# Half of the lower weight parts in the last four stages: from a VectorE subtraction to an accumulating transfer

## The chip, the cores and the metric

The kernel runs on one core of a Trainium2 chip. The metric is the device time of one execution in microseconds (us). The kernel before took 1247.65 us, the median of two runs (1247.44 and 1247.87).

## The reference

One decoder layer on 256 tokens of 2048 features in float32. After an rmsnorm, one wide projection `w_in` feeds a gated convolution branch, a gated linear attention branch with 4 heads and a cross attention into 256 memory tokens. Each branch ends in a projection of its own, is weighted with a sigmoid gate, and the sum goes through `w_out`, the residual and a last rmsnorm:

```
y_conv = (u * silu(conv_z)) @ w_conv_out + b_conv_out
y_gla  = (o * silu(gla_z)) @ w_gla_out
y_mem  = (om * silu(mz)) @ w_mem_out
g = sigmoid(gate_pre + b_gate)          # three gates per feature, from w_in
y = g[0] * y_conv + g[1] * y_gla + g[2] * y_mem
x = x + y @ w_out
return rmsnorm(x, final_g)
```

Nearly all arithmetic is in products of 256 token rows with weight matrices, some 235 MB of float32 weights in all, each read once.

## The kernel before

**Weights and their split.** The host lays the weights out in memory in the order in which the kernel asks for them. A *chunk* is 2 tiles of 128 input features by 512 output columns: 128 partitions of 4 KB, 512 KB in all. `chunk` (L123) loads it into `raw` by a transfer on SP's queue (L139), ScalarE rounds it to its upper 12 significant bits, `hi` (L140, type fp32r), and VectorE subtracts, `lo = raw - hi` (L141). The activations are split in the same way. `mm3` (L157) then makes three matmuls for each product, (upper, upper), (upper, lower) and (lower, upper), lines L158 to L160.

**Buffers.** There are 4 `raw` buffers (NRAW) and 5 each of `hi` and `lo` (NHL). A `hi` or `lo` buffer comes free when the matmuls of the chunk five before are done; a `raw` buffer when its subtraction is done. A few chunks of the last group (`spare=True`) take `hi` and `lo` from another pool.

**Order.** The order on each engine is made by the framework's scheduler, from program order and a simulated timeline. The three lines of a chunk have a raised priority (`tc.high_priority(offset=AHEAD)`, 400 instructions), so that loads and splits run as far ahead as buffers allow. Each engine, and each engine's queue of transfers, then runs its own list strictly in order: an instruction that waits holds up all that stand behind it.

**Groups and stages.** `group_t` (output features on partitions) makes 24 matmuls of 256 columns for a chunk, `group_n` (tokens on partitions) 12 of 512 columns. A group runs over 16 feature tiles, which are 8 chunks, k = 0, 2, ..., 14. Side work (convolution taps, attention heads, norms) is put between chunks. The last four stages, 128 of the chunks, have little of it:

- `cz`: 4 groups for conv_z, each followed by silu, a product and a split;
- `gc` and `yc`: in `merge`, in turn, 4 times one group for the gate (`gc`: bias, sigmoid) and one for `w_conv_out` (`yc`: bias, product, sum into `y`). After each pair `y` is transposed on TensorE and split;
- `out`: 4 groups for `w_out`. The residual `x` and `final_g` are loaded shortly before on SP's queue (L861, L864). In the last group the second half of the tokens runs 12 feature tiles behind the first, so that the end of the first half is covered; its chunks k = 4 and 6 are the `spare` ones.

GpSimd (POOL) issues no transfer in this kernel; it does a few memsets and powers.

Of the kernel before, what the change touches and what calls it, by code (L numbers as in the profile page):

```python
# [8 lines left out]
F32 = mybir.dt.float32  # L9
F32R = mybir.dt.float32r  # L10
U8 = mybir.dt.uint8
AF = mybir.ActivationFunctionType
ALU = mybir.AluOpType
# [3 lines left out]
P = 128  # L17
# [5 lines left out]
CK = 2  # L23
# [25 lines left out]

# columns of the packed per-feature vectors  # L50
V_LN, V_MLN, V_CG, V_CB, V_DB, V_GN, V_BA = 0, 16, 32, 48, 64, 80, 96
# [4 lines left out]
def trunk_kernel(ctx, tc, streamed, xt, memt, x, weights, w_alpha2, vecs, taps, b_gate, b_conv_out,  # L56
# [25 lines left out]

    # ---- side work: generators that are advanced between the chunks of weights. They yield how much
    # work they gave the vector engine, or ("wait", n) to go on n chunks later. ----
    class Side:
# [4 lines left out]
    def start(gen, rank=1):  # L90
        """Tasks of a lower rank go first."""
        task = [gen, 0, rank]
        at = len(Side.queue)
        while at and Side.queue[at - 1][2] > rank:
            at -= 1
        Side.queue.insert(at, task)
        return task
# [26 lines left out]

# [1 line left out]
    def chunk(w, k, a, cols, name, spare=False):  # L126
        """Rows of a tiles of 128 features from tile k on, cols: (first, count) side by side. The weights
        lie in memory in the order in which they are asked for."""
        b = sum(n for _, n in cols)
        at = sum(P * a * sum(n for _, n in cols) for _, _, a, cols in streamed)  # L130
        streamed.append((w, k, a, cols))
        raw = wp.tile([P, a, b], F32, name=f"raw_{name}", tag="raw", bufs=NRAW)
        if spare:
            hi, lo = b4([P, a, b], f"hi_{name}", F32R), b4([P, a, b], f"lo_{name}", F32R)
        else:
            hi = wp.tile([P, a, b], F32R, name=f"hi_{name}", tag="hi", bufs=NHL)
            lo = wp.tile([P, a, b], F32R, name=f"lo_{name}", tag="lo", bufs=NHL)
        with tc.high_priority(offset=AHEAD):
            nc.sync.dma_start(raw, weights[at:at + P * a * b].rearrange("(p k c) -> p k c", p=P, k=a))  # L139
            nc.scalar.copy(hi, raw)  # L140
            nc.vector.tensor_sub(lo, raw, hi.bitcast(F32))  # L141
        return hi, lo
# [19 lines left out]
    def group_t(w, c0, acts, nk, name, first=CK):  # L162
        """Output features on partitions: two tiles of [128, 2, tokens]."""
        pss = [mm_tile(f"pt_{name}_{j}") for j in range(2)]
        for k, hi, lo, ah, al in chunks(w, c0, nk, acts, name, first):
            for n in range(4):
                cols = slice(n * P, (n + 1) * P)
                mm3(pss[n // 2][:, (n % 2) * T:(n % 2 + 1) * T], hi[:, cols], lo[:, cols], ah, al,
                    k == 0 and n % 2 == 0, k == nk - 1)
        return [p.rearrange("p (a b) -> p a b", a=2) for p in pss]  # L170

    def group_n(w, c0, acts, nk, name):
        """Tokens on partitions: one tile of [128, 512], or of the columns, per token tile."""
        n = sum(c[1] for c in c0) if isinstance(c0, list) else GC
        pss = [mm_tile(f"pn_{name}_{t}")[:, 0:n] for t in range(NT)]
        for k, hi, lo, ah, al in chunks(w, c0, nk, acts, name):
            for t in range(NT):
                tok = slice(t * P, (t + 1) * P)
                mm3(pss[t], ah[:, tok], al[:, tok], hi, lo, k == 0, k == nk - 1)
        return pss  # L180
# [9 lines left out]
    def quarters(hi, lo):  # L190
        """Operands of 16 tiles of 128 features, four to a tile of SBUF."""
        return lambda k: (hi[k // 4][:, k % 4, :], lo[k // 4][:, k % 4, :])

    def rms_scale(ss, n, name, w=1):
        """(ss / n + EPS) ** -0.5"""
        ms = tp.tile([P, w], F32, name=f"ms_{name}", tag="ms")
        nc.vector.tensor_scalar(ms, ss, 1.0 / n, EPS, op0=ALU.mult, op1=ALU.add)
        rs = tp.tile([P, w], F32, name=f"rs_{name}", tag="rs")
        nc.gpsimd.tensor_tensor(rs, ms, mhalf[:, 0:w], op=ALU.pow)
        return rs  # L200

    def token_bcast(col, r, name):
        """[tokens, 1] per token tile -> r, [128, tokens], the same row on each partition."""
        pt = aux_tile(f"bc_{name}")
        for t in range(NT):
            dg = t1([P, P], f"dg_{name}_{t}")
            nc.vector.tensor_scalar_mul(dg, ident, col[:, t:t + 1])
            nc.tensor.matmul(pt[:, t * P:(t + 1) * P], lhsT=ones, rhs=dg, start=True, stop=True,
                             skip_group_check=True)
        nc.vector.tensor_copy(r, pt[:, 0:T])  # L210

    def feat_sum(src, name):
        """Sum over partitions of [128, tokens] -> PSUM [tokens, 1] per token tile."""
        pt = aux_tile(f"fs_{name}")
# [5 lines left out]
    def square_sum(part, src, name, squared=False):  # L220
        """part (or None) + the sum of squares over the 4 feature tiles of src."""
        sq = src
# [8 lines left out]

# [1 line left out]
    ones = const.tile([P, P], F32, name="ones")  # L233
# [14 lines left out]

# [1 line left out]
    def raw_operand(src, v0, name, keep):  # L250
        """Loads and splits as it is asked for: the operands, the loaded tiles or their squares."""
        hi, lo, raw, rest = [], [], [], []
# [71 lines left out]

# [1 line left out]
    conv = []  # L326
# [72 lines left out]
    def silu_psum(pz, name):  # L399
        """silu of a PSUM tile."""  # L400
        sg = t2([P, GC], f"sz_{name}")
# [5 lines left out]

# [1 line left out]
    cum = []  # L409

    def decay(alr):
        """alr: per token tile the low-rank inputs, in columns 0 and 64 on the upper, 32 on the lower bits."""
        wa = b4([P, 1024], "wa")
# [15 lines left out]
        for i in range(2):  # L429
            zb = b4([P, 4 * T], f"zb{i}")  # L430
            e = b4([P, 4 * T], f"lse{i}")
            for h in range(2):
# [9 lines left out]
                yield 0.7  # L442
            # log_sigmoid(z) = min(z, 0) - ln(1 + exp(-|z|)); sums inside chunks of TAU * log_a
            nc.scalar.activation(e, zb, AF.Abs)
# [24 lines left out]
    def gla_head(h, q, k, v):  # L469
        """q, k: [128, 2, tokens] of the head, q scaled; v: per token tile [128, 512]."""  # L470
        while len(cum) <= h:
# [3 lines left out]
        qf = q.rearrange("p a b -> p (a b)")  # L475
        # Scores are made as [key, query] for the two token tiles at once. The second tile has its keys
        # in reverse order, so that in each block its lower half lies where the first has its upper one.
        ck = b4([P, 4 * T], f"ck{h}")
# [11 lines left out]
        s1 = t1([P, P], f"s1{h}")  # L490
        # the diagonal, where nothing decays, and pairs of neighbours, where only the query does
        qq = b4([P, 4, P + CHUNK], f"qq{h}")
# [31 lines left out]

        # key in the lower and query in the upper half of a block of 2 L tokens: both decays
        # are taken to the end of the lower half, so that no exponent is positive
        made = []
        for li, L in list(enumerate(LEVELS))[1:]:
# [18 lines left out]
            if len(made) > LAG:  # L547
                level_scores(*made.pop(0))
                yield 0.2
        # key in the first, query in the second half of the sequence  # L550
        kd = t1([P, 2, P], f"kd{h}")
# [28 lines left out]
        yield "wait", 2  # L580
        # o = scores @ v, and its rmsnorm
        ov = b4([P, NT, DVH], f"on{h}")
# [35 lines left out]
    def v_group(h, q, k):  # L618
# [5 lines left out]
        else:  # L624
            # together with the low-rank inputs of the decays
            n = (DVH + RANK) // 2
# [15 lines left out]

# [1 line left out]
    def memory_groups():  # L644
# [77 lines left out]

# [1 line left out]
    def gated_gla():  # L724
        """The normalized o times silu(z), transposed, times the gain of the norm, split."""
        hi, lo = [], []
# [41 lines left out]

# [1 line left out]
    y = []  # L770
# [40 lines left out]

# [1 line left out]
    norm = start(x_norm())  # L813
# [41 lines left out]

# [1 line left out]
    res = []  # L857
# [8 lines left out]
    def residual(po, n, t):  # L866
        """Adds x; the mean of the squares goes to fss, the gain of the final norm to res."""
        half = slice(n % 2 * GC, (n % 2 + 1) * GC)
# [32 lines left out]

    # the last columns: the second token tile ends HELD feature tiles after the first
    pss = [mm_tile(f"pn_out3_{t}") for t in range(NT)]
# [59 lines left out]
```

## Time and profile before

| what | value |
|---|---|
| median of the runs | 1247.65 us |
| lowest and highest run | 1247.44, 1247.87 us |
| span of the profiled execution | 1246.8 us |
| TensorE (PE) busy | 1231.0 us, 99% |
| VectorE (DVE) busy | 964.0 us, 77% |
| ScalarE (ACT) busy | 591.8 us, 47% |
| GpSimd (POOL) busy | 18.6 us, 1% |
| mean share of the 16 DMA engines | some 57%, 191 GB/s |
| HBM read | 235.06 MB |

No time of its own is given for the profiled execution beside its span; the two runs lie 0.6 and 1.1 us above the span, which is the start and the end around it. Busy times are shares of the whole span and average over unlike stages. A matmul's record is longer than the step to the next matmul, since matmuls overlap, so a full PE row says that work was always in flight, not how fast it was.

### The profile page before, as it was taken

How to read it: one execution, taken by the hardware profiler on the slowest of the kernel's cores; microseconds unless marked ns; L12 is line 12 of the kernel's file. 1: busy time of each engine (PE TensorE's matmuls, PEld its weight loads, DVE VectorE, ACT ScalarE, POOL GpSimd, SP SyncE). 2: the span in 40 equal slices, each digit the busy share in tenths (PEclk: the TensorE clock that was granted, in tenths of full speed). 3: DMA queues.
4: the chain of work that ended last, by engine and by line, in shares of the span. 5: the costliest groups of instructions: out<-in, count | busy, mean ns of one | idle time of the engine just before them, and what ended most of it. 6: DMA issues, size and time to landing. Idle time of an engine off the chain costs nothing.

```text
span 1246.8 us, 18825 instructions
## 1 busy us (share of the span) xinstructions
PE 1231.0 (99%) x7338; PEld 1093.9 (88%) x7338; DVE 964.0 (77%) x1502; ACT 591.8 (47%) x711; POOL 18.6 (1%) x29
## 2 busy tenths in 40 slices
PE   7999999999999999999999999999999999999997
PEld 7999899988998998889988888888999888888885
DVE  7999999699999667999699979964565554655553
ACT  7534676446553454444445445544354444444442
POOL 0000000000020000000000000000000000000000
PEclk9999999999999999999999999999999999999999
DMA  7565745446545445665465555565555655567562
GB/s 272 186 191 170 236 153 195 155 161 221 188 165 193 159 152 183 205 204 193 161 218 171 200 201 171 179 228 194 195 183 190 202 202 195 205 227 268 187 215 71
DMA packets 71672, 238.37 MB, mean 191 GB/s; under 512 B 7792, under 2 KB 12144, under 8 KB 71584
## 3 DMA queue, kind: packets, MB, share of 16 engines
q1 hardware_dynamic: 71440, 237.13, 56.6%
q8 instruction: 57, 0.93, 0.3%
q14 instruction: 31, 0.25, 0.1%
q10 hardware_dynamic: 144, 0.05, 0.0%
HBM read 235.06 MB, written 2.10 MB: 190 GB/s over the span
## 4 chain that ended last, share of the span: by engine, by line
PE 97%; DMA 1%; DVE 1%; issue 0%; SPq 0%; ACT 0%; POOLq 0%; DVEq 0%; POOL 0%
PE pt_cb L158 2%; PE pt_cz L158 2%; PE pt_cb L159 2%; PE pt_cb L160 2%; PE pt_cz L159 2%; PE pt_cz L160 2%; PE pn_gc L159 2%; PE pn_gm L159 2%; PE pn_gz L158 2%; PE pn_go L159 2%; PE pn_go L158 2%; PE pn_gm L158 2%; PE pn_gz L159 2%; PE pn_yo L158 2%; PE pn_go L160 2%; PE pn_gc L160 2%
## 5 line engine op out<-in xcount | busy, mean ns | idle before, releaser
L359 DVE SCALAR_TENSOR_TENSOR conv<-u,tap,conv 128x256 f32<-128x256 f32 x480 | 207.3, 474 | 0.0
L158 PE MATMUL pt_ca<-xh,hi_ca 128*128 128x256 f32 x256 | 72.7, 289 | 6.1 <-ACT xh L187 5.1
L159 PE MATMUL pt_ca<-xl,hi_ca 128*128 128x256 f32 x256 | 73.5, 288 | 0.2
L160 PE MATMUL pt_ca<-xh,lo_ca 128*128 128x256 f32 x256 | 72.7, 287 | 0.9 <-DVE lo_ca L141 0.9
L158 PE MATMUL pt_cb<-xh,hi_cb 128*128 128x256 f32 x256 | 72.4, 283 | 0.0
L141 DVE TENSOR_TENSOR lo_yc<-raw_yc,hi_yc 128x1024 fp32r<-128x1024 f32 x32 | 39.2, 1225 | 42.9 <-ACT hi_yc L140 42.9
L160 PE MATMUL pt_cz<-xh,lo_cz 128*128 128x256 f32 x256 | 71.9, 281 | 0.0
L158 PE MATMUL pt_cz<-xh,hi_cz 128*128 128x256 f32 x256 | 71.9, 281 | 0.0
L159 PE MATMUL pt_cz<-xl,hi_cz 128*128 128x256 f32 x256 | 71.9, 281 | 0.0
L160 PE MATMUL pt_cb<-xh,lo_cb 128*128 128x256 f32 x256 | 71.8, 282 | 0.0
L159 PE MATMUL pt_cb<-xl,hi_cb 128*128 128x256 f32 x256 | 71.8, 281 | 0.0
L141 DVE TENSOR_TENSOR lo_cz<-raw_cz,hi_cz 128x1024 fp32r<-128x1024 f32 x32 | 39.2, 1224 | 35.7 <-ACT hi_cz L140 35.7
L141 DVE TENSOR_TENSOR lo_gc<-raw_gc,hi_gc 128x1024 fp32r<-128x1024 f32 x32 | 39.1, 1223 | 34.2 <-ACT hi_gc L140 34.2
L141 DVE TENSOR_TENSOR lo_out<-raw_out,hi_out 128x1024 fp32r<-128x1024 f32 x32 | 39.0, 1224 | 31.5 <-ACT hi_out L140 31.2
L140 ACT CAST hi_gc<-raw_gc 128x1024 fp32r<-128x1024 f32 x32 | 33.6, 1052 | 50.3 <-PE pn_yc L160 24.9
L140 ACT CAST hi_yc<-raw_yc 128x1024 fp32r<-128x1024 f32 x32 | 33.7, 1053 | 49.5 <-PE pn_gc L160 33.4
L140 ACT CAST hi_yo<-raw_yo 128x1024 fp32r<-128x1024 f32 x32 | 33.6, 1051 | 46.7 <-PE pn_go L160 23.4
L141 DVE TENSOR_TENSOR lo_yo<-raw_yo,hi_yo 128x1024 fp32r<-128x1024 f32 x32 | 38.8, 1221 | 21.6 <-ACT hi_yo L140 21.6
L158 PEld LDWEIGHTS pt_ca<-xh,hi_ca 128*128 128x128 f32 x256 | 49.5, 196 | 6.4 <-ACT xh L187 5.1
L140 ACT CAST hi_gm<-raw_gm 128x1024 fp32r<-128x1024 f32 x32 | 33.6, 1050 | 45.2 <-PE pn_gm L160 24.6
L140 ACT CAST hi_go<-raw_go 128x1024 fp32r<-128x1024 f32 x32 | 33.7, 1052 | 44.6 <-PE pn_yo L160 24.6
L140 ACT CAST hi_cz<-raw_cz 128x1024 fp32r<-128x1024 f32 x32 | 33.6, 1050 | 44.3 <-PE pt_cz L159 36.0
(352 smaller groups left out, 4108.9 us busy)
## 6 DMA issues: line engine op xcount, KB each, us to landing
raw_cb<-in_weights SPq DMA_DIRECT2D x32, 512.0 KB, 3.5
raw_gm<-in_weights SPq DMA_DIRECT2D x32, 512.0 KB, 3.2
raw_gz<-in_weights SPq DMA_DIRECT2D x32, 512.0 KB, 3.3
raw_go<-in_weights SPq DMA_DIRECT2D x32, 512.0 KB, 3.6
raw_yo<-in_weights SPq DMA_DIRECT2D x32, 512.0 KB, 3.2
raw_cz<-in_weights SPq DMA_DIRECT2D x32, 512.0 KB, 3.2
raw_gc<-in_weights SPq DMA_DIRECT2D x32, 512.0 KB, 3.2
raw_yc<-in_weights SPq DMA_DIRECT2D x32, 512.0 KB, 3.2
```

Source lines behind the costliest of these rows:

```text
L140: nc.scalar.copy(hi, raw)
L141: nc.vector.tensor_sub(lo, raw, hi.bitcast(F32))
L158: nc.tensor.matmul(o, lhsT=ah, rhs=bh, start=first, stop=False, skip_group_check=True)
L159: nc.tensor.matmul(o, lhsT=ah, rhs=bl, start=False, stop=False, skip_group_check=True)
L160: nc.tensor.matmul(o, lhsT=al, rhs=bh, start=False, stop=last, skip_group_check=True)
L359: nc.vector.scalar_tensor_tensor(acc, u[:, i, j:j + T], tap[:, c, j:j + 1], acc, op0=ALU.mult, op1=ALU.add)
```

## The change

`lo_by` names, for the four last stages, the chunks with k divisible by 4, which is every second one (k = 0, 4, 8, 12 of each group). In `gc` and `out` ("twice") such a chunk is loaded by a transfer from GpSimd's queue straight into `hi`, with the conversion to fp32r on the way; ScalarE writes `lo = -hi`; then a second transfer from GpSimd's queue reads the same weights again and adds them to `lo`. In `cz` and `yc` ("once") `raw` is loaded and `hi` made as before, ScalarE writes `lo = -raw` in fp32r, and a transfer from GpSimd's queue adds the weights to `lo`. A `spare` chunk stays as it was. All other lines of the diff take out comments.

```
+    def lo_by(name, k):
+        if k % (2 * CK):
+            return None
+        if name.startswith(("gc", "out")):
+            return "twice"
+        if name.startswith(("cz", "yc")):
+            return "once"
+        return None
...
     def chunk(w, k, a, cols, name, spare=False):
...
+        src = weights[at:at + P * a * b].rearrange("(p k c) -> p k c", p=P, k=a)
+        how = lo_by(name, k)
+        if how and not spare:
+            hi = wp.tile([P, a, b], F32R, name=f"hi_{name}", tag="hi", bufs=NHL)
+            lo = wp.tile([P, a, b], F32R, name=f"lo_{name}", tag="lo", bufs=NHL)
+            with tc.high_priority(offset=AHEAD):
+                if how == "twice":
+                    nc.gpsimd.dma_start(hi, src)
+                    nc.scalar.activation(lo, hi.bitcast(F32), AF.Copy, scale=-1.0)
+                else:
+                    raw = wp.tile([P, a, b], F32, name=f"raw_{name}", tag="raw", bufs=NRAW)
+                    nc.sync.dma_start(raw, src)
+                    nc.scalar.copy(hi, raw)
+                    nc.scalar.activation(lo, raw, AF.Copy, scale=-1.0)
+                nc.gpsimd.dma_start(lo, src, accum_op=ALU.add)
+            return hi, lo
         raw = wp.tile([P, a, b], F32, name=f"raw_{name}", tag="raw", bufs=NRAW)
...
-            nc.sync.dma_start(raw, weights[at:at + P * a * b].rearrange("(p k c) -> p k c", p=P, k=a))
+            nc.sync.dma_start(raw, src)
             nc.scalar.copy(hi, raw)
             nc.vector.tensor_sub(lo, raw, hi.bitcast(F32))
         return hi, lo
```

## Rows read from the trace of the kernel before

**Rows 1.** The page: busy time of engines; then the chain that ended last, by engine.
```profile
PE 1231.0 (99%) x7338; PEld 1093.9 (88%) x7338; DVE 964.0 (77%) x1502; ACT 591.8 (47%) x711; POOL 18.6 (1%) x29
...
PE 97%; DMA 1%; DVE 1%; issue 0%; SPq 0%; ACT 0%; POOLq 0%; DVEq 0%; POOL 0%
```

**Rows 2.** Busy time by windows: three stretches of loads, then four short ones.
```profile
core 0: us, PE busy (x) PEld busy (x) DVE busy (x) ACT busy (x) POOL busy (x), PEclk, DMA share, GB/s
862.00:972.00 110.00, 110.00 (x854) 106.53 (x854) 61.65 (x62) 48.36 (x54) 0.00 (x0) 1.00 0.56 189
972.00:1150.00 178.00, 178.00 (x798) 147.03 (x797) 100.74 (x103) 76.85 (x82) 0.00 (x0) 1.00 0.64 218
1150.00:1219.00 69.00, 69.00 (x310) 57.23 (x309) 43.55 (x46) 32.98 (x41) 0.00 (x0) 1.00 0.57 192
1115.00:1126.00 11.00, 11.00 (x51) 9.06 (x49) 6.10 (x6) 4.36 (x6) 0.00 (x0) 1.00 0.96 339
1137.00:1148.00 11.00, 11.00 (x50) 9.13 (x49) 4.90 (x4) 4.38 (x5) 0.00 (x0) 1.00 0.79 290
1126.00:1137.00 11.00, 11.00 (x50) 9.04 (x50) 6.10 (x6) 5.29 (x7) 0.00 (x0) 1.00 0.79 244
1060.00:1071.00 11.00, 11.00 (x54) 9.14 (x53) 8.36 (x11) 4.87 (x6) 0.00 (x0) 1.00 0.64 222
```

**Rows 3.** The page's groups: busy us, mean ns | idle before, its releaser; the split.
```profile
L141 DVE TENSOR_TENSOR lo_yc<-raw_yc,hi_yc 128x1024 fp32r<-128x1024 f32 x32 | 39.2, 1225 | 42.9 <-ACT hi_yc L140 42.9
...
L141 DVE TENSOR_TENSOR lo_gc<-raw_gc,hi_gc 128x1024 fp32r<-128x1024 f32 x32 | 39.1, 1223 | 34.2 <-ACT hi_gc L140 34.2
...
L140 ACT CAST hi_gc<-raw_gc 128x1024 fp32r<-128x1024 f32 x32 | 33.6, 1052 | 50.3 <-PE pn_yc L160 24.9
```

**Rows 4.** Timeline (start, length, idle before): casts, a subtraction, and the matmul that uses lo.
```profile
983.69 1.05 ACT L140 CAST hi_yc<-raw_yc 128x1024 fp32r<-128x1024 f32 x1 [1.70 <-PE pn_gc L160]
984.77 1.23 DVE L141 TENSOR_TENSOR lo_yc<-raw_yc,hi_yc 128x1024 fp32r<-128x1024 f32 x1 [1.52 <-ACT hi_yc L140]
986.43 1.05 ACT L140 CAST hi_yc<-raw_yc 128x1024 fp32r<-128x1024 f32 x1 [1.70 <-PE pn_gc L160]
...
994.66 0.39 PE L159 MATMUL pn_yc<-lo_yc,uh 128*128 128x512 f32 x1
```

**Rows 5.** Tile raw_gc: issue on SP (ns min/median/max), and its transfers' landing.
```profile
L139 SPq DMA_DIRECT2D raw_gc<-in_weights x32: 327/328/328, 952.5 to 1105.3; - x32
...
DMA to landing us min/median/max: 3.1/3.2/4.3
```

**Rows 6.** Tile raw_yc: the same.
```profile
L139 SPq DMA_DIRECT2D raw_yc<-in_weights x32: 327/328/328, 975.1 to 1128.1; - x32
...
DMA to landing us min/median/max: 3.0/3.2/6.8
```

**Rows 7.** SP's waits, 862 to 1220 us: total us, times, longest.
```profile
SPq L139 <- DVE lo_gc L141: 71.7, 32, 2.6
SPq L139 <- DVE lo_yc L141: 69.8, 31, 3.2
```

**Rows 8.** GpSimd's groups from 862 us to the end.
```profile
L890 POOL TENSOR_TENSOR frs<-fms,mhalf 128x1 f32<-128x1 f32 x2 | 1.1, 540 | 0.2
L889 POOL TENSOR_TENSOR fms<-fs,fss 128x1 f32<-128x1 f32 x2 | 0.4, 190 | 459.6 <-ACT fsq L872 459.6
```

## The prediction

> **What bounds the kernel now.** I read the busy line and the chain that ended last first: TensorE is busy 99% of the span and carries 97% of the chain [rows 1]. Then the windows of the last four stages: from 862 to 1219 us TensorE is busy in every microsecond at granted clock 1.00, while VectorE is busy 55 to 63% [rows 2]. No group of matmuls there waits for a weight. So the 1.22 us subtraction that the change removes [rows 3] is hidden today, with room: ScalarE starts a cast at 983.69, as soon as a buffer of five chunks before is free, and the matmul that reads the lower part of that chunk starts at 994.66, 10.97 us later [rows 4]; cast and subtraction need 1.05 + 1.22 of that. VectorE leaving this work can give TensorE nothing. The question is only whether what takes its place stays hidden too: in the same 10.97 us, and in what the DMA engines have left.
>
> **What goes.** Of 128 chunks in the four stages, every second is changed, less the one that is spare: 63 (16 in cz, 16 in yc, 16 in gc, 15 in out). 63 subtractions of 1.22 us leave VectorE, 77 us, off the path: worth 0. In the 31 "twice" chunks the SP issue and the raw buffer go too. SP's loads wait for the subtraction that frees a raw buffer, 71.7 us in 32 waits for gc [rows 7]; with half of the raw chunks gone there, SP runs further ahead. That saves nothing either, but pushes plain loads against the new transfers. The odd chunks keep the cast and the subtraction.
>
> **What comes on ScalarE.** "Twice": one negation in the place of the cast, same shape, so 1.05 us for 1.05 us [rows 3]; it waits for a landing rather than for TensorE. Behind it in ScalarE's list stands the cast of the next odd chunk, and behind that VectorE's subtraction. If it starts the 3.2 us of a landing late [rows 5], it still has 10.97 - 2.27 - 3.2 = 5.5 us. "Once": one more pass of 1.05 us, 32 times, 34 us in stretches where ScalarE is busy 43 to 48% [rows 2]. Worth 0; if that cover failed, at most those 34 us.
>
> **What comes as a wait.** A "twice" chunk now needs: landing of hi 3.2 us [rows 5], negation 1.05, landing of the accumulating transfer, and 0.1 us for each of three wake-ups (an estimate: the subtraction starts 0.03 us after its cast has ended [rows 4]). No row shows an accumulating transfer. Below, it is like a copy, 3.2 us; nothing excludes less, but a gain in landing would be worth nothing. Above, the slowest load of yc, 6.8 us [rows 6]. I take 3.2 plus the time of reading another 0.524 MB at the full rate worked out below (353 GB/s), 1.5 us, since it must read lo as well as the weights: 4.7. The sum is 3.2 + 1.05 + 4.7 + 0.3 = 9.3 of 10.97: hidden, by 1.7 us only. With 6.8 it is 11.4, and late. A "once" chunk needs 1.05 + 1.05 + 4.7 + 0.3 = 7.1, hidden. The queue is the other wait: GpSimd has nothing else to do here (its groups come at the very end [rows 8]), but it issues in order, and the accumulating transfer waits for ScalarE in front of the next chunk's hi load. One round is landing 3.2 + negation 1.05 + an issue 0.33 (SP's, [rows 5]) + two wake-ups 0.2 = 4.8 us, against 5.56 us for two chunks (178 us for 32 pairs, [rows 2]). Also hidden, by 0.8 us. The Trainium skill (DMA: Bandwidth & Descriptors, Specifications) gives a transfer from GpSimd about 1 us to the first byte where SP's takes 0.6; by its 0.4 us more for each of two, a round would be 5.6 us and just not fit, which makes some 1 us over 31 rounds. No run here shows it yet.
>
> **What comes on the DMA engines.** This is where I expect the time. From 862 to 1219 us they move 110 x 189 + 178 x 218 + 69 x 192 GB/s x us = 20.8 + 38.8 + 13.2 = 72.8 MB [rows 2]. What is their full rate? The densest stretch moves 339 GB/s at a share of 0.96, so 353 at 1.00; other stretches give 290/0.79 = 367, 222/0.64 = 347 and 244/0.79 = 309 [rows 2]. I take 353, from the row that is nearest to full. The change reads 63 x 0.524 = 33.0 MB of weights a second time, and each accumulating transfer also reads the 0.524 MB that lie in lo, another 33.0 MB. Lower bound: the reading of lo is free; then 105.8 MB / 353 = 300 us of 357, a share of 0.84, and nothing is lost. Upper bound: it counts in full, at 309 GB/s: 138.8 / 309 = 449 us, 92 more. I take it in full at 353, since a transfer that reads two streams and writes one cannot pass its engine at the rate of a copy. By stage: cz 20.8 + 16.8 = 37.6 MB, 106 us of 110, fits. gc and yc 38.8 + 33.6 = 72.4 MB, 205 us for 178: +27. out 13.2 + 15.7 = 28.9 MB, 82 us for 69: +13. Of the sum of 40 some 8 us are paid from the lead: the first weights of yc are asked for at 975.1 [rows 6], 19.6 us ahead of their matmul [rows 4], and in a stage that waits for its loads a landing, a chain and a chunk are enough, some 11 to 12. Net +32. The Trainium skill (Collectives: The Full Stack, Part 3) puts the cost of an adding transfer in its two source reads on one ring and gives copy against add as 62.28 to 32.35, a factor of 1.93; by that the extra would be 63.7 instead of 66.0 MB, 2.3 / 0.353 = 6.5 us less at most, and the sum +26. No row of before shows it.
>
> The terms are made against the span of 1246.8 us; the median of the runs, 1247.65, is 0.85 above it and I add to the median: 1247.65 + 32 = 1279.7, **1280 us**.
>
> **The rivals.**
> - *A, the forecast: the DMA engines become the bound.* 21 us (at 367 GB/s, before the lead) to 92 us over, 1260 to 1340. For: 0.64 of the share is taken in gc and yc already [rows 2]. Against: no row shows an adding transfer, nor a share held at 1.00.
> - *B, not slower: all of it is hidden.* Place: the same transfers. It decides if an adding transfer takes the engines little longer than a copy: up to 357 x 353 = 126 MB fit, so if less than 20 of the 33 MB of lo's reading count. Price 0, at most a few us where the loads of x bunch (share 0.96): 1245 to 1255. For: each chain above fits by 0.8 to 1.7 us, and TensorE has 10.97 us of lead. The Trainium skill (DMA: Bandwidth & Descriptors, Bandwidth) gives 425 GB/s for one 16 MB transfer, by which even the 138.8 MB would take 327 us of 357; against it, the densest stretch here moves 339 at 0.96.
> - *C, slower by the queue and not by the engines.* The in-order round on GpSimd binds once a hi load lands in over 4.0 us (5.56 - 1.55). At 4.3 us, gc's slowest [rows 5], it costs 0.3 x 31 = 9 us; at 6.8 [rows 6], 2.8 x 31 = 87: 1257 to 1335. For: landings stretch under load, as those two maxima show, and GpSimd's own issue is in no row. Against: the scheduler may put the next hi load ahead.
> - *D, the change does not do what it says*: if the hi load does not round, lo is zero, and all times are as in A to C; it needs no price of its own.
>
> **How the numbers follow.** A 0.46, B 0.30, C 0.22, a gain 0.02 (only by a better order, which the full TensorE rows leave no room for). 2% is 25 us, and about what a measurement of this kernel can tell from no change. Of A, 0.09 lies under 25 us, of C 0.04. Within 2%: 0.30 + 0.09 + 0.04 = 0.43. Slower: 0.37 + 0.18 = 0.55. Faster: 0.02. The range takes in B from 1246 and A and C to 1325, which leaves out some 0.03 below and 0.12 above. A's own range is 1260 to 1325.
>
> **What would show it.** In A: DMA share of 0.95 or more from 972 to 1219 us, TensorE idle before the matmuls that read lo, with its transfer as releaser, in yc as much as in gc, and cz hardly longer. In B: TensorE full, share near 0.84. In C: share under 0.9, idle in gc and out but not in cz and yc, and GpSimd's queue waiting for ScalarE's negation. The mean landing of an accumulating transfer tells the middle term: 4.7 us by my sum. The prediction is wrong if TensorE stays without gaps, or if cz alone loses over 10 us.

## The result and the profile after

The changed kernel takes 1306.45 us (median of 1305.41 and 1307.48) against 1247.65: a ratio of 1.0473, 95% interval 1.0442 to 1.0503, or 59 us more. The profiled execution has a span of 1303.6 us, 56.8 more than before. (Line numbers are 26 higher than before: L166 and L167 are the cast and the subtraction, L184 to L186 the matmuls.)

The busy line and the DMA queues of the page of the changed kernel, to be read beside [rows 1]:

```profile
PE 1249.2 (96%) x7338; PEld 1100.6 (84%) x7338; DVE 889.6 (68%) x1439; ACT 618.6 (47%) x743; POOL 91.7 (7%) x123
...
q1 hardware_dynamic: 66976, 220.88, 49.5%
q0 software_dynamic: 13536, 49.29, 17.8%
```

VectorE is rid of 74 us and TensorE does the same 7338 matmuls. Queue q0 is GpSimd's: 49.29 MB are the 31 loads of hi and the 63 adding transfers, 0.524 MB each, so that the reading of lo isn't counted in MB. The same columns as [rows 2], by stage (cz with its lead, gc with yc, out), and then the part of out in which SP still loads weights, to 1260 us:

```profile
862.00:972.00 110.00, 109.93 (x854) 106.22 (x853) 38.84 (x43) 62.59 (x68) 16.52 (x20) 1.00 0.95 264
972.00:1183.00 211.00, 190.26 (x791) 152.62 (x792) 63.63 (x72) 88.82 (x97) 36.73 (x48) 0.95 0.94 264
1183.00:1295.00 112.00, 93.94 (x392) 74.02 (x391) 32.97 (x43) 36.40 (x46) 20.50 (x29) 0.97 0.78 194
1183.00:1260.00 77.00, 61.16 (x253) 47.62 (x253) 24.25 (x28) 27.27 (x33) 15.98 (x22) 0.97 0.89 226
```

cz loses nothing at a share of 0.95. gc with yc takes 211 us for 178, at 0.94; out loses the most for its length and takes 112 us for 88. The share of 0.78 there takes in the end of the stage, when SP has no more to load; up to there it is 0.89. So the share is highest in the stage that loses nothing, which speaks against full DMA engines as the cause but does not rule them out. TensorE's waits in that run (in total, times, longest) name the place:

```profile
PE pn_gc L185 <- DMA lo_gc<-in_weights: 20.7, 11, 3.0
PE pn_out L185 <- DMA lo_out<-in_weights: 18.0, 9, 4.3
```

All are for the adding transfer of "twice" chunks, none for cz or yc, and none for the odd chunks, whose casts stand behind the negations in ScalarE's list. The granted clock fell too, to a mean of 0.95 and 0.97 (1.00 is 2.4 GHz; the lower level is 1.2). It fell in the stages in which TensorE stood idle, and 5% of 211 and 3% of 112 us are some 14 us beside the 39 of the waits (an estimate from these two means); together that is 53 of the 57 us.

The landings answer to [rows 5, 6]. The view of tile hi_gc in the changed kernel has the load's issue (ns min/median/max), the negation and the load's landing:

```profile
L149 POOL DMA_DIRECT2D hi_gc<-in_weights x16: 561/567/892, 960.3 to 1135.1; - x16
...
L150 ACT ACTIVATE lo_gc<-hi_gc x16: 1053/1059/1062, 967.1 to 1148.0; 128x1024 fp32r<-128x1024 f32 x16
...
DMA to landing us min/median/max: 5.0/6.8/12.9
```

The view of tile lo_gc has the same of the adding transfer:

```profile
L156 POOL DMA_DIRECT2D lo_gc<-in_weights x16: 868/876/899, 968.5 to 1149.4; - x16
...
DMA to landing us min/median/max: 5.2/5.4/10.8
```

And that of tile lo_cz its landing in cz, beside more loads of SP:

```profile
DMA to landing us min/median/max: 7.4/8.0/8.8
```

The load of hi in gc lands in 6.8 us where I had put 3.2. One "twice" chunk of out, followed through the timeline of the changed kernel:

```profile
1215.05 0.62 POOL L149 DMA_DIRECT2D hi_out<-in_weights  x1
...
1221.97 1.06 ACT L150 ACTIVATE lo_out<-hi_out 128x1024 fp32r<-128x1024 f32 x1 [2.94 <-DMA hi_out<-in_weights]
...
1223.33 0.89 POOL L156 DMA_DIRECT2D lo_out<-in_weights  x1 [1.97 <-ACT lo_out L150]
...
1228.63 0.50 PE L185 MATMUL pn_out<-lo_out,yh 128*128 128x512 f32 x1 [2.24 <-DMA lo_out<-in_weights]
```

Its buffer came free at about 1213.2. The load was issued 1.8 later, behind another adding transfer; landing and negation by 1223.03, the second issue at 1223.33, and TensorE, idle for 2.24, starts at 1228.63: 15.4 us from free to use, where the buffers give 10.97 [rows 4]. Over the 21 "twice" chunks of gc and out whose start is in these stages (the fourth group of out left aside, since its order differs) the same five steps are, on average: 0.93 until the issue, 6.83 to the landing, 0.34 to the negation, 1.40 to the second issue, 6.18 to its landing: **15.68 us**. (Over all 28 "twice" chunks ahead of the fourth group of out the mean is 15.73.)

What such a chain costs can be worked out. The *lead* is the time that the buffers give: a chunk's buffer comes free four chunks before TensorE wants the chunk, 10.97 us when nothing waits. With five buffers a changed chunk waits for the buffer of an unchanged one, and six chunks lie from one late chunk to the next that it can make late. So each six chunks lose what the chain is longer than the lead: 64 chunks / 6 x (15.68 - 10.97) = 50 us. (For a late chunk the chain ends where TensorE's wait does, so this sum in good part counts the same waits in another way; that it comes near 59 shows where the time went, and the experiments have to show why.) This is **theory C1**: the lost time is the chain beyond the lead of the buffers. Its rivals are **A**, the forecast (the DMA engines are the bound), and **C2**, my rival C (the queue in order on GpSimd, where loads and adding transfers hold each other up).

### The profile page after: what moved, and what is told of

The parts are those of the page before. It is cut to its first block, busy times and chain, and to the rows that moved or that the text cites. A ratio compares the mean times of both kernels' runs of the same rounds, so it can differ in the third digit from the quotient of the medians.

```text
span 1303.6 us, 18920 instructions
## 1 busy us (share of the span) xinstructions
PE 1249.2 (96%) x7338; PEld 1100.6 (84%) x7338; DVE 889.6 (68%) x1439; ACT 618.6 (47%) x743; POOL 91.7 (7%) x123
## 3 DMA queue, kind: packets, MB, share of 16 engines
q0 software_dynamic: 13536, 49.29, 17.8%
## 4 chain that ended last, share of the span: by engine, by line
PE 67%; issue 22%; POOL 4%; DMA 3%; DVE 1%; ACT 1%; SPq 0%; POOLq 0%; DVEq 0%; ACTq 0%
PE pt_cb L184 2%; PE pt_cb L185 2%; PE pt_cb L186 2%; PE pn_gm L185 2%; PE pn_gz L184 2%; PE pn_go L185 2%; PE pn_go L184 2%; PE pn_gm L184 2%; PE pn_gz L185 2%; PE pn_go L186 2%; PE pn_gz L186 2%; PE pn_gm L186 2%; PE pn_yo L184 2%; PE pn_yo L185 2%; PE pn_yo L186 2%
## 5 line engine op out<-in xcount | busy, mean ns | idle before, releaser
L184 PE MATMUL pt_ca<-xh,hi_ca 128*128 128x256 f32 x256 | 72.3, 288 | 5.4 <-ACT xh L213 4.8
L185 PE MATMUL pn_gc<-lo_gc,xh 128*128 128x512 f32 x128 | 55.5, 433 | 20.8 <-DMA lo_gc<-in_weights 20.7
L186 PE MATMUL pt_ca<-xh,lo_ca 128*128 128x256 f32 x256 | 72.3, 286 | 1.2 <-DVE lo_ca L167 1.2
L184 PE MATMUL pt_cb<-xh,hi_cb 128*128 128x256 f32 x256 | 72.4, 283 | 0.0
L186 PE MATMUL pt_cz<-xh,lo_cz 128*128 128x256 f32 x256 | 71.9, 281 | 0.0
L184 PE MATMUL pt_cz<-xh,hi_cz 128*128 128x256 f32 x256 | 71.9, 281 | 0.0
L186 PE MATMUL pt_cb<-xh,lo_cb 128*128 128x256 f32 x256 | 71.8, 282 | 0.0
L167 DVE TENSOR_TENSOR lo_yc<-raw_yc,hi_yc 128x1024 fp32r<-128x1024 f32 x16 | 19.6, 1226 | 75.2 <-ACT hi_yc L166 75.2
L185 PE MATMUL pn_out<-lo_out,yh 128*128 128x512 f32 x128 | 52.6, 411 | 18.1 <-DMA lo_out<-in_weights 18.0
L167 DVE TENSOR_TENSOR lo_out<-raw_out,hi_out 128x1024 fp32r<-128x1024 f32 x17 | 20.7, 1225 | 70.5 <-ACT hi_out L166 70.5
L166 ACT CAST hi_yo<-raw_yo 128x1024 fp32r<-128x1024 f32 x32 | 33.6, 1051 | 46.4 <-PE pn_go L186 21.7
L166 ACT CAST hi_gm<-raw_gm 128x1024 fp32r<-128x1024 f32 x32 | 33.6, 1050 | 45.2 <-PE pn_gm L186 24.6
L166 ACT CAST hi_go<-raw_go 128x1024 fp32r<-128x1024 f32 x32 | 33.6, 1052 | 44.6 <-PE pn_yo L186 24.7
L167 DVE TENSOR_TENSOR lo_cz<-raw_cz,hi_cz 128x1024 fp32r<-128x1024 f32 x16 | 19.6, 1224 | 51.6 <-ACT hi_cz L166 51.6
L166 ACT CAST hi_gz<-raw_gz 128x1024 fp32r<-128x1024 f32 x32 | 33.7, 1052 | 43.7 <-PE pn_gz L186 32.8
L184 PEld LDWEIGHTS pt_ca<-xh,hi_ca 128*128 128x128 f32 x256 | 49.2, 194 | 5.8 <-ACT xh L213 4.8
L186 PE MATMUL pn_gc<-hi_gc,xl 128*128 128x512 f32 x128 | 53.9, 421 | 0.0
L167 DVE TENSOR_TENSOR lo_yo<-raw_yo,hi_yo 128x1024 fp32r<-128x1024 f32 x32 | 38.9, 1225 | 21.6 <-ACT hi_yo L166 21.6
```

Of the source, the lines that this page charges most:

```text
L184: nc.tensor.matmul(o, lhsT=ah, rhs=bh, start=first, stop=False, skip_group_check=True)
L185: nc.tensor.matmul(o, lhsT=ah, rhs=bl, start=False, stop=False, skip_group_check=True)
L186: nc.tensor.matmul(o, lhsT=al, rhs=bh, start=False, stop=last, skip_group_check=True)
```

## The experiments

Each kernel is the changed one with the edit shown, except where it says otherwise; each ran beside the kernel before, and the ratio is to that.

**1. Everything "once".**

```
-        if name.startswith(("gc", "out")):
-            return "twice"
-        if name.startswith(("cz", "yc")):
+        if name.startswith(("gc", "out", "cz", "yc")):
             return "once"
```

> gc and out chunks are made like those of cz and yc (raw by SP, cast and negation on ScalarE, adding transfer on GpSimd's queue): the same bytes are read, no load of hi on GpSimd's queue. Theory A (the DMA engines are the bound): no shorter than the changed kernel, 1295 to 1315 us, TensorE waits in gc, yc and out. Theory C (the chain hi landing, negation, adding transfer, in one queue and in the 10.97 us that the buffers give): most of the loss goes, 1248 to 1268 us, at a DMA share that stays at 0.95 or more.

1255.57 us, ratio 1.0065 (1.005 to 1.008). The DMA queues of its page:

```profile
q1 hardware_dynamic: 71440, 237.13, 53.9%
q0 software_dynamic: 9072, 33.03, 14.0%
```

Two of the stretches of [rows 2] in this run:

```profile
972.00:1150.00 178.00, 174.68 (x775) 142.76 (x774) 60.10 (x68) 101.78 (x110) 27.05 (x31) 1.00 1.02 297
1150.00:1219.00 69.00, 65.39 (x284) 53.39 (x284) 23.55 (x28) 39.80 (x47) 10.49 (x12) 0.98 1.00 290
```

The landing of lo_gc in this run:

```profile
DMA to landing us min/median/max: 8.2/8.4/9.8
```

The same bytes, the engines full at 1.00 to 1.02 (the profile's share can come out a little over 1, as here), adding transfers of gc that land in 8.4 us instead of 5.4, and 51 of the 59 us are gone. Theory A is worth at most the 8 us that are left. The reason is in the chain, which here is negation and adding transfer alone: 10.45 us on average over 41 chunks, inside 10.97. The engines' time for one 0.524 MB is 53.9% of 1255.9 us / (237.13 / 0.524) = 1.50 us for a plain load and 14.0% of 1255.9 / 63 = 2.79 us for an adding one, a factor of 1.86. The Trainium skill (Collectives: The Full Stack, Part 3) has 62.28 GB/s for copying against 32.35 for adding, a factor of 1.93, measured in a ring of four ranks and not for loads into SBUF; the 1.86 here is near it.

**2. Only cz and yc changed.**

```
-        if name.startswith(("gc", "out")):
-            return "twice"
```

> Only cz and yc are changed, gc and out are as before. A: yc runs at the engines' limit but gc beside it has room, 1247 to 1256 us. C: no chain with a load in it, 1247 to 1250 us. Both: cz shows a share near 0.99 and no wait.

1248.17 us, 1.0004 (0.9995 to 1.0014), with no wait of TensorE in these stages. 32 chunks by adding transfer cost nothing, and gain nothing. Both theories had that. The share in cz was 0.95 and not near the 0.99 expected.

**3. Only gc and out changed.**

```
-        if name.startswith(("cz", "yc")):
-            return "once"
```

> Only gc and out are changed, cz and yc are as before, so that 16.8 MB of adding transfers leave cz and as many leave yc. A: gc and out need some 5 to 10% more of the engines than there is, 1255 to 1270 us. C: the chain is unchanged but for shorter landings, 1285 to 1306 us, TensorE's waits in gc and out alone.

1299.25 us, 1.0396 (1.0354 to 1.0438): 51 of the 59 us with half of the adding transfers. The stretch of gc with yc in this run:

```profile
972.00:1150.00 178.00, 163.84 (x699) 132.94 (x700) 73.78 (x78) 66.41 (x72) 20.19 (x29) 0.96 0.80 231
```

Its DMA issues in gc (KB each, median us to landing):

```profile
raw_gc<-in_weights SPq DMA_DIRECT2D x16, 512.0 KB, 3.2
hi_gc<-in_weights POOLq DMA_DIRECT2D x16, 512.0 KB, 6.5
lo_gc<-in_weights POOLq DMA_DIRECT2D x16, 512.0 KB, 6.7
```

A full fifth of the engines is idle and the chain is as long as before, 15.73 us. A's 1255 to 1270 is out. Under C I had expected shorter landings; they did not come (hi 6.5 for 6.8 us in gc, lo 6.7 for 5.4).

The trace of this run also says something on why hi lands late. Of the 31 loads of hi in gc and out, 11 were issued with no adding transfer under way in GpSimd's queue: they landed in 5.1 us (median). 15 were issued 0.6 to 1.2 us behind an adding transfer, with nothing but adding transfers under way: they landed in 7.8, each 1.2 to 2.8 us after the adding transfer ahead of it, while SP's loads of gc took 3.2.

**4. No addition.** The second transfer copies over lo, so lo is not the lower part here.

```
-                nc.gpsimd.dma_start(lo, src, accum_op=ALU.add)
+                nc.gpsimd.dma_start(lo, src)
```

> The second transfer copies the weights over lo instead of adding them (lo is not the lower part then): same transfers, queues and waits, but no reading of lo. A: the engines get back what lo's reading took, share under 0.88, 1247 to 1262 us. C: the last link of the chain and, through less load, the hi landing get shorter by 1 to 2 us each; the chain is then 11 to 12 us against 10.97, 1255 to 1280 us. The landings of lo against those of the changed kernel (8.0 us in cz) price the addition.

1273.61 us, 1.0216 (1.0193 to 1.0239). Its DMA issues:

```profile
lo_cz<-in_weights POOLq DMA_DIRECT2D x16, 512.0 KB, 4.7
...
hi_gc<-in_weights POOLq DMA_DIRECT2D x16, 512.0 KB, 5.6
lo_gc<-in_weights POOLq DMA_DIRECT2D x16, 512.0 KB, 4.8
```

The copy lands 3.3 us earlier than the addition in cz (8.0), and takes the chain in gc and out to 12.90: still 1.9 late, as C1 had it. A's 1247 to 1262 is out here too, with a share of 0.86 from 972 to 1150 us.

**5. Raw chunks loaded by GpSimd.** Experiment 1, with this edit for gc and out:

```
-                    nc.sync.dma_start(raw, src)
+                    (nc.gpsimd if name.startswith(("gc", "out")) else nc.sync).dma_start(raw, src)
```

> As in e1_all_once (1255.57 us), but the raw chunks of gc and out that get an adding transfer are loaded by GpSimd's queue instead of SP's. So loads and adding transfers share one queue in order again, as in the changed kernel, but a load goes to a raw buffer well ahead and is no link of the chain. Theory C1 (the chain is longer than the lead of the buffers): the chain stays cast, negation, adding transfer, 1252 to 1262 us. Theory C2 (the queue in order holds up loads and additions): 1270 to 1300 us, TensorE waits for lo_gc and lo_out.

1253.15 us, 1.0045 (1.003 to 1.006). Loads and additions in one queue, in order, cost nothing more than in experiment 1, as long as the load isn't a link of the chain. So C2 falls as a cause by itself. Inside the chain of the changed kernel the queue does have a part: of the 0.93 us until the issue 0.30 are there on a free queue, which leaves 0.6 of the 4.7 us that the chain is late, and by the landings of experiment 3 some more lies in the landing of a load that stands behind an adding transfer. No run separates that part.

**6 and 7. Six buffers, and their control.** In the changed kernel and in the kernel before:

```
-NB4, NB2, NB1, NRAW, NHL = 19, 8, 8, 4, 5
+NB4, NB2, NB1, NRAW, NHL = 19, 6, 8, 3, 6
```

> The changed kernel with 6 hi and 6 lo buffers instead of 5, paid for with 3 raw buffers for 4 and 6 tiles for 8 in one pool of temporaries. The chain then has 13.7 instead of 10.97 us, the queue is as it was. C1: most of the loss of 59 us goes, 1255 to 1280 us. C2 and A: unchanged, 1295 to 1310 us.

> Control for e6: the kernel before with the same buffer counts. All theories: within 0.5% of the kernel before, 1246 to 1254 us; what it loses is to be taken off e6.

1320.77 us, 1.0574 (1.0554 to 1.0593), and 1256.2 us, 1.0067 (1.0052 to 1.0082) for the control. This miss went against C1: a longer lead did not help. The chain had grown to 18.31 us, more than the lead (13.69). Some of ScalarE's waits in this run show loads that come late with 3 raw buffers:

```profile
ACT lo_gc L150 <- DMA hi_gc<-in_weights: 64.7, 14, 12.1
ACT hi_cb L166 <- DMA raw_cb<-in_weights: 32.2, 18, 4.1
```

**8. Every fourth chunk.**

```
-        if k % (2 * CK):
+        if k % (4 * CK):
```

> Only every fourth chunk is changed (k = 0 and 8 of each group): 32 instead of 63. C1: each twice chunk is still late, by less since landings are shorter under less load, 1254 to 1275 us. C2: a round of the queue has 11 us instead of 5.5 and fits, 1247 to 1252 us. A: share near 0.8, 1247 to 1250 us.

1278.43 us, 1.0238 (1.0218 to 1.0259): half the changed chunks, half the loss. Neither the engines (0.80 from 972 to 1150 us) nor a round of the queue, which has 11 us here instead of 5.5, can explain it; the chain, 14.28 us, can. C2 as a round of the queue is out here too, and C1's range ended 3 us short of the result.

**9. The hi load alone.** cz and yc as before; in gc and out:

```
                 if how == "twice":
+                    raw = wp.tile([P, a, b], F32, name=f"raw_{name}", tag="raw", bufs=NRAW)
+                    nc.sync.dma_start(raw, src)
                     nc.gpsimd.dma_start(hi, src)
-                    nc.scalar.activation(lo, hi.bitcast(F32), AF.Copy, scale=-1.0)
+                    nc.vector.tensor_sub(lo, raw, hi.bitcast(F32))
+                    return hi, lo
```

> Only gc and out differ from the kernel before: every second chunk gets hi by a load on GpSimd's queue and raw by SP, and VectorE subtracts as before; no negation and no adding transfer. The same bytes are read from HBM as in e3_only_twice. Theory C1 (lost time is what the chain of a chunk takes beyond the lead of its buffers): the chain is hi landing, some 6 us, and a subtraction of 1.2, 7.5 of 10.97 us, so nothing is lost: 1246 to 1252 us. If loads on GpSimd's queue are themselves the trouble: over 1265 us.

1248.53 us, 1.001 (1.0001 to 1.002). The stretch of gc with yc in this run:

```profile
972.00:1150.00 178.00, 178.00 (x796) 147.07 (x795) 100.31 (x104) 58.73 (x64) 8.64 (x16) 1.00 0.78 263
```

Its DMA issues in gc:

```profile
raw_gc<-in_weights SPq DMA_DIRECT2D x32, 512.0 KB, 4.4
hi_gc<-in_weights POOLq DMA_DIRECT2D x16, 512.0 KB, 4.7
```

A load on GpSimd's queue with a short chain behind it is hidden. In gc it lands 0.3 us later than SP's, in out 0.1 us sooner (5.9 and 6.0). The Trainium skill (DMA: Bandwidth & Descriptors, Specifications) gives about 1 us to the first byte for GpSimd's transfers and about 0.6 for SP's; no run here shows first bytes, and of that 0.4 the landings show 0.3 in gc and nothing in out.

**10 and 11. Four buffers, and their control.** Experiment 1 and the kernel before, with:

```
-NB4, NB2, NB1, NRAW, NHL = 19, 8, 8, 4, 5
+NB4, NB2, NB1, NRAW, NHL = 19, 8, 8, 4, 4
```

> e1_all_once (1255.57 us) with 4 hi and 4 lo buffers for 5. The bytes and queues are the same, the lead falls from 10.97 to 8.2 us. Its chain took 10.45 us on average there. C1: 1 to 2.3 us late, now on every fourth chunk since four buffers lead from changed chunk to changed chunk: 128 / 4 x 1.0 to 2.3 = 32 to 74 us, 1285 to 1330 us, TensorE waits for lo in all four stages. Theory A (only the DMA engines count): 1250 to 1260 us as in e1.

> Control for e10: the kernel before with 4 hi and 4 lo buffers. C1: cast and subtraction take 2.4 of 8.2 us, 1246 to 1252 us.

1291.53 us, 1.0354 (1.0339 to 1.037), and 1249.28, 1.0017 (1.0007 to 1.0026). TensorE's waits in experiment 10:

```profile
PE pt_cz L184 <- DMA lo_cz<-in_weights: 11.6, 12, 2.3
PE pn_yc L183 <- DMA lo_yc<-in_weights: 8.8, 7, 2.8
PE pn_gc L183 <- DMA lo_gc<-in_weights: 5.0, 6, 1.4
PE pn_out L183 <- DMA lo_out<-in_weights: 4.7, 6, 2.1
```

Only the lead is shorter, and a kernel that had lost 8 us loses 44, now in all four stages. With the chain that it had, 9.56 us, C1 gives 128 / 4 x (9.56 - 8.25) = 42 us. (Over all changed chunks ahead of the fourth group of out the mean chain is 9.8 us, which gives 50, so the sum is good to some 8 us.) This is the plainest of the tests.

**12. Six buffers with all raw buffers,** to settle experiment 6.

```
-NB4, NB2, NB1, NRAW, NHL = 19, 8, 8, 4, 5
+NB4, NB2, NB1, NRAW, NHL = 19, 6, 4, 4, 6
```

> e6 again, with all 4 raw buffers: the sixth hi and lo buffer are paid for from two pools of temporaries (6 for 8 and 4 for 8 tiles), so that stages before cz may lose some us. Read by stage: gc with yc took 211.5 us and out 112 in the changed kernel, 177.7 and 88 before. If e6 failed because its 3 raw buffers made the loads late: C1 holds, the chain of 15.7 us against a lead of 13.7 loses 64 / 6 x 2.0 = 21 us, gc with yc and out take 275 to 300 us together. If six buffers only put more transfers in flight, so that the landings grow with the lead: 310 to 335 us together, a chain near 18 us.

1293.01 us, 1.0368 (1.0349 to 1.0388). gc with yc took 205.6 us and out 105.6, 311 together (before the change 266, in the changed kernel 323.5). The 311 lie in the range of the second reading (landings that grow with the lead), at its lower edge. The 3 raw buffers were a good deal of the miss in 6 (28 us less with 4, though the pools of temporaries differ too, and this run has no control), but with them restored the chain is 17.19 us, longer by 1.5 than with five buffers, and eats over half of the 2.72 us that the sixth buffer adds.

Worked-out loss against measured, by C1 (chain - lead, per cycle of chunks):

```
                      chain  lead  chunks/cycle  worked out  measured, us
changed kernel        15.68  10.97     64/6        50          59
3  gc and out only    15.73  10.97     64/6        51          51
4  no addition        12.90  10.97     64/6        21          26
8  every fourth       14.28  10.97     64/8        26          31
10 once, 4 buffers     9.56   8.25    128/4        42          44
12 six buffers        17.19  13.69     64/6        37          45
6  six, 3 raw         18.31  13.69     64/6        49          73
1  all once           10.45  10.97       -          0           8
```

What is measured above the worked-out loss is 8 to 9 us where the engines are full (the changed kernel as in 1), nothing in 3, 2 to 5 in runs 4, 8 and 10, 8 in 12, and 24 in 6, whose control had lost 9 by itself. These rests were not taken apart; the lower clock after waits is one candidate.

## Why the prediction was right, and where it was not

- **What bounds the kernel, and what leaves it.** Right: TensorE gained nothing from 74 us less of VectorE, cz takes what it took, and all of the loss lies in gc with yc and in out.
- **The direction and the range.** Right, 1306 in 1246 to 1325, and slower by more than 2%; 26 us over the point, so the loss was 1.84 times the +32 that I gave. That it fell into the range is in good part luck: the upper part of the range was priced for full engines (A) and for a round of the queue (C), and the loss came by the chain, which the prediction called hidden.
- **"What comes on the DMA engines": the mechanism I chose fell.** I expected +32 us from full engines; they cost at most 8 (experiment 1). The step that failed is the full rate. I took 353 GB/s from the densest stretch, counting the reading of lo in the bytes. At a share of 1.02 experiment 1 moves 297 GB/s as counted, and beside that reads some 31 x 0.524 MB of lo in 178 us, 91 GB/s: 388 in all. With 388, 138.8 MB need 358 us where 357 were there, which goes with the few us that experiment 1 lost. The price of an addition (two transfers' worth of engine time) was right.
- **"What comes as a wait": the term that was mis-sized.** I called the chain hidden by 1.7 us: 9.3 = 3.2 + 1.05 + 4.7 + 0.3. It measured 15.7. The negation was right at 1.06; both landings were taken too short. 3.2 was SP's median without this load, and 6.83 was measured; 4.7 was that with an extra reading, and 6.18 was measured. Issues and wake-ups were 0.93 + 0.34 + 0.34 and not 0.3 (an issue on GpSimd's queue takes 0.57 for the load and 0.88 for the addition). The slowest landing on record, 6.8 [rows 6], went into one link only: with 6.8 in both links the sum would have been 15, and late. The sum for a "once" chunk, 7.1, was too short as well: 10.45 was measured in experiment 1, hidden by 0.5 us only. Where the change itself makes the load, a slow landing is to be reckoned with in every link.
- **The rivals.** C had the right chunks (gc and out, not cz and yc, TensorE waiting for an addition), but as a round of the queue, at 87 us for landings of 6.8; experiments 5 and 8 speak against the round. It was not how the queue ran, either: the next load of hi was often issued ahead of the adding transfer that waited (at 1220.80, between the two issues of the chunk above), as the prediction's "against" had it. And the round counted one issue of 0.33 us where two took 0.57 and 0.88. What decides is the plain sum of the chain against the lead, which I had written down and dismissed. B holds where the chain is short: experiments 2 and 9 lose nothing.
- **What would show it.** Of my signs, "idle in gc and out but not in cz and yc" was C's and true; "share of 0.95 or more" was A's and nearly true as well, in cz and gc. A's sign of idle time in yc as much as in gc was not there. A full share alone decided nothing; experiment 1 at 1.02 is 51 us faster than the changed kernel at 0.89 to 0.95. The landing of an adding transfer, which was to tell the middle term (4.7), came out at 5.4 (gc) to 8.8 (yc).

That the lists in order on ScalarE (the cast of a later chunk stands ahead of many a negation) add little is seen from the 0.34 us between landing and negation. Why exactly the landing of hi grows is open: the landings of experiment 3 point at the adding transfers ahead of it in its queue, but it wasn't tried with the two in different queues, nor with the engines' load changed alone.

## What to carry to other kernels

When work is moved from an engine to a chain of transfers, add up the chain from the moment its buffer comes free to the first use, with landings as they are under the load that the change makes, and hold that against (buffers - 1) steps of the consumer; what is over is lost once for each cycle of buffers that links late chunks. A load into a buffer of another pool, which starts well ahead of the cycle as the raw load does in experiments 1 and 5, costs little even with the DMA engines full; the same bytes as links of the chain cost 51 us. More buffers are not a sure cure: with a sixth the chain itself grew by 1.5 us (experiment 12). That more transfers in flight land later is the likely reason, but it was not tested by itself.

## What was not expected of the hardware

- A GpSimd load of 512 KB in gc lands in 4.7 us beside SP loads alone (experiment 9, share 0.78) and in 6.5 when adding transfers go through the same queue (experiment 3, share 0.80), while SP's loads of gc land in 3.2 there. In experiment 3 a load issued just behind an adding transfer lands 1.2 to 2.8 us after it.
- An adding transfer took the engines 2.79 us against 1.50 for a plain load (experiment 1, both as means over the whole run), and landed in 8.0 us against 4.7 for a copy in its place (cz, changed kernel against experiment 4).
- In experiment 1 the engines held a share of 0.97 to 1.02 from 862 to 1219 us, and the kernel lost only 8 us by it.
